# Relative-bias rows replicated by eight DRAM-to-DRAM copies instead of one transfer out of SBUF, in a one-core decoder step

## The chip, the core and the metric

One core of one Trainium2 chip runs the whole program as one launch. The metric is the device time in microseconds; each measured number is one execution, and the program before was run three times: 2370.03, 2372.45 and 2373.29 us, median 2372.45 us.

## What is computed

One layer of a decoder trunk for 1024 prompt tokens and 8 sample tokens (1032 in all), model width 1024. The part that matters here is the first feed-forward step and, much later, a table of biases:

```
h = layer_norm(ALPHA * x + 0.5 * swiglu(x, ffn1_wg, ffn1_wu, ffn1_wd), ln1_g, ln1_b)
...
def swiglu(x, wg, wu, wd):
    return (jax.nn.silu(x @ wg) * (x @ wu)) @ wd
...
bias = rel_bias[t5_bucket(qpos[None, :, None] - idx)].astype(jnp.float32)
logits = logits + bias.transpose(0, 3, 1, 2)
```

`rel_bias` has 32 buckets for each of 8 heads. The bias depends on the distance between query and key alone.

## The kernel before, in words

Everything is computed transposed: features on the partitions, tokens in the free dimension, in three chunks of 344 tokens. Products are made from three matmuls each (high part by high, high by low, low by high), so each weight of 128x1024 (512 KB) is loaded by SP, cast by ScalarE into a high part (L273) and subtracted by VectorE into a low part (L274).

The first feed-forward step runs in two passes. `chunk0` (L416) takes the first 344 tokens through all 22 blocks of the hidden width: `plain` (L369) makes 24 matmuls for the gate (`pg_f`) and 24 for the up projection (`pu_f`), then `down` (L396) multiplies two blocks at a time into eight 128x344 tiles, which VectorE adds to `z` (L407). `chunks12` (L512) then takes the other two chunks together. Beside the first part of `chunk0`, `load_x` (L701) loads x in nine tiles of 128 tokens into three buffers (`xn0` to `xn8`, L710), TensorE transposes each tile (L721), ScalarE and VectorE split the result (L731, L732) and ScalarE copies it into `z` (L736). `load_x` counts the tiles in `g.xb`.

Also in this stretch `bias_rows` (L1253) makes the bias table: TensorE multiplies `rel_bias` with a one-hot matrix (L1262), ScalarE copies the 8x384 result to eight partitions of SBUF (L1264), and one DMA (L1265) writes it to DRAM as `scr`, each head's row of 384 numbers 128 times, 1536 KB. It is read again at L1491, after 1100 us, by an access pattern that shifts each of the 128 rows by one element, which gives the tile of biases of a head.

Order: the Python code runs many generators beside each other, with a clock of its own (`Sched`, L43); a generator yields the time until it wants to go on. Tiles in the pool `ap` share 24 numbered buffers (`A`, L98), which `Free` gives out. Behind that, the framework's scheduler lays down the final order on each engine; it may take an instruction whose inputs are ready ahead of one written earlier. Every engine, SP's DMA queue among them, runs its instructions strictly in that order. `params` (L1943) releases the buffers of the parameters and of the bias.

Of the kernel before, what the change touches and what calls it, by code (L numbers as in the profile page):

```python
# [15 lines left out]
F32 = mybir.dt.float32  # L16
# [69 lines left out]
def bank(g, kind, name):  # L86

    ks = g.banks[kind]
    t = g.ps.tile([P, 512], F32, tag=f"b{ks[g.bi[kind] % len(ks)]}", name=name, bufs=1)
    g.bi[kind] += 1  # L90
    return t
# [6 lines left out]
def A(g, slot, name, dt=F32, n=NTOK):  # L98

    return g.ap.tile([P, n], dt, tag=f"a{slot}", name=name, bufs=1)  # L100
# [1149 lines left out]

def bias_rows(g, rel_bias, oh, scr):  # L1253

    nc = g.nc
    ta = A(g, 20, "bra")
    rb, oht, row = ta[0:32, 0:8], ta[0:32, 8:392], ta[0:8, 400:784]
    nc.sync.dma_start(rb, rel_bias)
    nc.sync.dma_start(oht, oh)
    yield 6.0  # L1260
    ps = bank(g, 'aux', "bt")
    nc.tensor.matmul(ps[0:8, 0:384], rb, oht, start=True, stop=True)  # L1262
    g.s.t += 0.7
    nc.scalar.copy(row, ps[0:8, 0:384])  # L1264
    nc.sync.dma_start(scr, row.unsqueeze(1).broadcast_to((8, 128, 384)))  # L1265


class Pair:
# [615 lines left out]
def trunk(tc, i, o):  # L1884
    nc = tc.nc
    g = G()
    g.nc, g.tc, g.s = nc, tc, Sched()
    s = g.s
# [4 lines left out]
    dp = S_("dp", space=bass.MemoryType.DRAM)  # L1893
# [44 lines left out]
    for j, k in enumerate(ln):  # L1938
        nc.sync.dma_start(prow[8 * j:8 * j + 8], i[k][0].rearrange("(k p) -> k p", p=P))
    nc.sync.dma_start(prow[32:36], i['ret_gn_g'][0].rearrange("(h p) -> h p", p=P))  # L1940
    br = s.add(bias_rows(g, i['rel_bias'], i['oh'], g.scr), 6.0)

    def params():  # L1943

        pp = bank(g, 'aux', "prm")
        nc.tensor.transpose(pp[:, 0:36], prow, g.ident[0:36, 0:36])
        nc.scalar.copy(prm, pp[:, 0:36])
        g.fs.put(21)
        while s.live(br):
            yield 1.0  # L1950
        yield 40.0
        g.fs.put(20)

    def widen():

# [2 lines left out]
        yield 0  # L1958

    s.add(params(), 20.0)  # L1960
    s.add(widen(), 6.0)
    psum = {}
# [31 lines left out]
    h = [None] * NCH  # L1994
# [495 lines left out]
```

## Time and profile before

| | |
|---|---|
| median of three runs | 2372.45 us (2370.03 to 2373.29) |
| the profiled execution | 2370.71 us, span 2368.9 us |
| TensorE busy (share of the span) | 2239.6 us (95%) |
| TensorE weight load busy | 2160.1 us (91%) |
| VectorE busy | 1772.9 us (75%) |
| ScalarE busy | 1076.6 us (45%) |
| GpSimd busy | 361.2 us (15%) |
| DMA moved | 224.40 MB, 95 GB/s on average |

All times of views are microseconds from the start of the span; the execution's own time is 1.81 us longer than the span. A stretch of 40 us near the start is under 2% of the span, so that shares over the whole span say little about it: it has to be read from windows of its own.

### The profile page before, as it was taken

What the parts mean: (1) busy time and instruction counts of PE and PEld (TensorE: products, weight loads), DVE (VectorE), ACT (ScalarE), POOL (GpSimd) and SP (SyncE); (2) the same over time, 40 slices, a digit from 0 to 9 for tenths busy, and PEclk for the clock granted to TensorE, in tenths of its full rate; (3) what the DMA queues carried; (4) which work ended last, traced back from release to release, by engine and by line L of the source; (5) the groups of instructions that cost most, each with busy time, mean ns of one, the idle gap of its engine ahead of it and who ended that gap; (6) DMA issues with size and microseconds to landing.
All of it is one profiled execution on the core that took longest, in us unless ns stands there. A gap on an engine that the chain in (4) does not pass through costs nothing.

```text
span 2368.9 us, 37153 instructions
## 1 busy us (share of the span) xinstructions
PE 2239.6 (95%) x14231; PEld 2160.1 (91%) x14231; DVE 1772.9 (75%) x3780; ACT 1076.6 (45%) x1944; POOL 361.2 (15%) x372
## 2 busy tenths in 40 slices
PE   8899999999999998899899999898999899999996
PEld 7899999999998998888689988787999899999995
DVE  4655688787878588777866678876578788887866
ACT  4433343333334466787466665342345443333331
POOL 0000100000002313454023233223220200000003
PEclk9999999999999999999999999998999999999998
DMA  6644322222222201121321242436644321222211
GB/s 176 208 143 142 119 84 81 81 73 71 81 79 101 71 23 51 50 83 47 90 74 49 57 151 72 146 90 153 190 128 145 110 81 63 90 72 74 87 54 48
DMA packets 239370, 224.40 MB, mean 95 GB/s; under 512 B 13291, under 2 KB 219959, under 8 KB 238423
## 3 DMA queue, kind: packets, MB, share of 16 engines
q1 hardware_dynamic: 234838, 209.36, 29.6%
q0 software_dynamic: 4352, 12.65, 2.3%
q8 instruction: 112, 1.84, 0.3%
q14 instruction: 68, 0.55, 0.1%
HBM read 199.40 MB, written 22.58 MB: 94 GB/s over the span
## 4 chain that ended last, share of the span: by engine, by line
PE 73%; DVE 11%; ACT 7%; DMA 3%; issue 3%; POOL 1%; another core or an unknown queue 1%; SPq 0%; POOLq 0%; DVEq 0%; ACTq 0%
PE pds_f L403 4%; PE pds_f L404 4%; PE pds_f L405 4%; ACT ja L1003 3%; PE pdp_f L403 2%; PE pg_f L171 2%; PE pg_f L169 2%; PE pg_f L170 2%; PE pdp_f L404 2%; PE pdp_f L405 2%; PE ps_f2U L169 2%; PE pu_f L169 2%; PE ps_f2U L170 2%; PE ps_f2U L171 2%; PE ps_f1U L169 2%
## 5 line engine op out<-in xcount | busy, mean ns | idle before, releaser
L407 DVE SCALAR_TENSOR_TENSOR z<-pds_f,z 128x344 f32<-128x344 f32 x320 | 164.4, 515 | 137.9 <-PE pds_f L405 137.4
L403 PE MATMUL pds_f<-gs_f,wh_f1ds 128*128 128x344 f32 x352 | 113.8, 324 | 1.7 <-DVE z L407 1.7
L404 PE MATMUL pds_f<-gs_f,wh_f1ds 128*128 128x344 f32 x352 | 113.1, 321 | 0.0
L403 PE MATMUL pds_f<-gs_f,wh_f2ds 128*128 128x344 f32 x352 | 113.0, 321 | 0.0
L404 PE MATMUL pds_f<-gs_f,wh_f2ds 128*128 128x344 f32 x352 | 113.0, 321 | 0.0
L405 PE MATMUL pds_f<-gs_f,wl_f2ds 128*128 128x344 f32 x352 | 112.8, 321 | 0.0
L405 PE MATMUL pds_f<-gs_f,wl_f1ds 128*128 128x344 f32 x352 | 112.7, 320 | 0.0
L407 DVE SCALAR_TENSOR_TENSOR z<-pdp_f,z 128x344 f32<-128x344 f32 x160 | 79.8, 511 | 43.2 <-PE pdp_f L405 42.6
L1003 ACT ACTIVATE ja<-key,zt 128x1024 bf16<-128x1024 int16 (+5 forms) x90 | 93.8, 1042 | 38.2 <-DVE zt L1014 31.0
L684 POOL TENSOR_TENSOR yt<-yt,lot 128x512 f32<-128x512 f32 (+1 forms) x7 | 7.2, 1040 | 548.5 <-DVE lot L677 530.9
L296 ACT CAST wS_f1G<-ws_f1G 128x512 fp32r<-128x512 f32 x44 | 25.1, 619 | 131.4 <-PE pds_f L404 95.2
L296 ACT CAST wS_f2G<-ws_f2G 128x512 fp32r<-128x512 f32 x44 | 25.2, 618 | 129.5 <-PE pds_f L405 120.9
L1468 ACT CAST p<-pT 128x512 fp32r<-128x512 f32 (+2 forms) x112 | 47.4, 433 | 55.8 <-PE pT L1464 43.4
L574 POOL TENSOR_TENSOR lns_l<-z 128x344 f32<-128x344 f32 x3 | 4.1, 1355 | 440.8 <-DVE z L407 430.3
L403 PEld LDWEIGHTS pds_f<-gs_f,wh_f1ds 128*128 128x128 f32 x352 | 66.5, 189 | 3.0 <-DVE z L407 2.2
L404 PEld LDWEIGHTS pds_f<-gs_f,wh_f1ds 128*128 128x128 f32 x352 | 66.5, 189 | 0.3 <-DVE gs_f L466 0.2
L403 PEld LDWEIGHTS pds_f<-gs_f,wh_f2ds 128*128 128x128 f32 x352 | 66.5, 189 | 0.2 <-ACT gs_f L465 0.2
L405 PEld LDWEIGHTS pds_f<-gs_f,wl_f2ds 128*128 128x128 f32 x352 | 66.5, 189 | 0.0
L404 PEld LDWEIGHTS pds_f<-gs_f,wh_f2ds 128*128 128x128 f32 x352 | 66.4, 189 | 0.0
L405 PEld LDWEIGHTS pds_f<-gs_f,wl_f1ds 128*128 128x128 f32 x352 | 66.5, 189 | 0.0
L403 PE MATMUL pdp_f<-gt_f,wh_f2dp 128*128 128x344 f32 x176 | 57.8, 328 | 3.9 <-issue 2.4
L1469 DVE TENSOR_TENSOR p<-pT,p 128x512 fp32r<-128x512 f32 (+2 forms) x112 | 54.4, 496 | 9.2 <-ACT p L1468 8.0
(806 smaller groups left out, 8729.2 us busy)
## 6 DMA issues: line engine op xcount, KB each, us to landing
wr_f1g<-in_ffn_wg_dram SPq DMA_DIRECT2D x22, 512.0 KB
wr_f1u<-in_ffn_wu_dram SPq DMA_DIRECT2D x22, 512.0 KB
wr_f1dp<-in_ffn_wd_dram SPq DMA_DIRECT2D x22, 512.0 KB
wr_f1G<-in_ffn_wg_dram SPq DMA_DIRECT2D x22, 512.0 KB
wr_f1U<-in_ffn_wu_dram SPq DMA_DIRECT2D x22, 512.0 KB
wr_f1ds<-in_ffn_wd_dram SPq DMA_DIRECT2D x22, 512.0 KB
wr_f2u<-in_ffn_wu_dram SPq DMA_DIRECT2D x22, 512.0 KB
wr_f2g<-in_ffn_wg_dram SPq DMA_DIRECT2D x22, 512.0 KB
```

The lines of the kernel that those rows point to most:

```text
L169: g.nc.tensor.matmul(ps, w[0][:, k, :], x[0][:, k, :], start=first and i == 0, stop=False)
L170: g.nc.tensor.matmul(ps, w[0][:, k, :], x[1][:, k, :], start=False, stop=False)
L171: g.nc.tensor.matmul(ps, w[1][:, k, :], x[0][:, k, :], start=False, stop=last and i == n - 1)
L296: nc.scalar.copy(t[:, 0], src)
L403: g.nc.tensor.matmul(ps, wh[:, o, :], th, start=i == 0, stop=False)
L404: g.nc.tensor.matmul(ps, wh[:, o, :], tl, start=False, stop=False)
L405: g.nc.tensor.matmul(ps, wl[:, o, :], th, start=False, stop=i == len(grp) - 1)
L407: g.nc.vector.scalar_tensor_tensor(out=z, in0=ps, scalar=0.5 / ALPHA, in1=z, op0=OP.mult, op1=OP.add)
L684: nc.gpsimd.tensor_tensor(out=yh, in0=yh, in1=mv[0:n, 0:1].broadcast_to((n, 512)), op=OP.subtract)
L1003: nc.scalar.activation(jk[:, 0:n], key[b], AF.Sign, bias=t[:, j:j + 1], scale=-1.0, accum_out=cnt[:, j:j + 1])
L1468: nc.scalar.copy(ph[:, js, ts], ptv[:, js, ts])
L1469: nc.vector.tensor_tensor(out=pl[:, js, ts], in0=ptv[:, js, ts], in1=ph[:, js, ts].bitcast(F32), op=OP.subtract)
```

## The change

`bias_rows` no longer writes the 1536 KB from SBUF. It stores the 8x384 result once to DRAM (`one`, the new tile `brow`) and then copies, head by head, from DRAM to DRAM: each copy reads one row of `brow` and writes it 128 times into `scr[h]`. In the code the copies come after a loop that waits for the ninth x tile, 12 units of the scheduler's clock apart. The buffer number 20 is now released by `bias_rows` itself.

```diff
-def bias_rows(g, rel_bias, oh, scr):
+def bias_rows(g, rel_bias, oh, one, scr):
...
     nc.scalar.copy(row, ps[0:8, 0:384])
-    nc.sync.dma_start(scr, row.unsqueeze(1).broadcast_to((8, 128, 384)))
+    nc.sync.dma_start(one, row)
+    yield 40.0
+    g.fs.put(20)
+    while g.xb < 9:
+        yield 1.0
+    yield 40.0
+    for h in range(8):
+        nc.sync.dma_start(scr[h], one[h:h + 1, :].broadcast_to((128, 384)))
+        yield 12.0
...
-    br = s.add(bias_rows(g, i['rel_bias'], i['oh'], g.scr), 6.0)
+    s.add(bias_rows(g, i['rel_bias'], i['oh'], dp.tile([8, 384], F32, name="brow"), g.scr), 6.0)
...
         g.fs.put(21)
-        while s.live(br):
-            yield 1.0
-        yield 40.0
-        g.fs.put(20)
+        yield 0
```

SP's queue, from the bias transfer on, before (`wr_f1g4` is the load of the gate weight of block 4, `u` the up and `dp` the down weight, `xn6` the seventh x tile):

```order
L1265 DMA scr_60<-bra_240 1024x1x384
L710 DMA xn6_335<-in_x_prompt_dram 128x1024
L228 DMA wr_f1g4_0_400<-in_ffn1_wg_dram 128x8x128
L228 DMA wr_f1u4_0_425<-in_ffn1_wu_dram 128x8x128
L710 DMA xn7_455<-in_x_prompt_dram 128x1024
L228 DMA wr_f1dp2_0_461<-in_ffn1_wd_dram 128x1024
L228 DMA wr_f1dp3_0_483<-in_ffn1_wd_dram 128x1024
L228 DMA wr_f1g5_0_505<-in_ffn1_wg_dram 128x8x128
L228 DMA wr_f1u5_0_527<-in_ffn1_wu_dram 128x8x128
L228 DMA wr_f1g6_0_548<-in_ffn1_wg_dram 128x8x128
```

and the same place of the same queue with the change:

```order
L1265 DMA brow_179<-bra_241 8x384
L228 DMA wr_f1g4_0_401<-in_ffn1_wg_dram 128x8x128
L710 DMA xn6_336<-in_x_prompt_dram 128x1024
L1272 DMA scr_60<-brow_179 128x384 x2
L228 DMA wr_f1g5_0_506<-in_ffn1_wg_dram 128x8x128
L228 DMA wr_f1u4_0_426<-in_ffn1_wu_dram 128x8x128
L228 DMA wr_f1dp2_0_462<-in_ffn1_wd_dram 128x1024
L228 DMA wr_f1dp3_0_484<-in_ffn1_wd_dram 128x1024
L1272 DMA scr_60<-brow_179 128x384 x3
L710 DMA xn7_456<-in_x_prompt_dram 128x1024
L228 DMA wr_f1u5_0_528<-in_ffn1_wu_dram 128x8x128
L1272 DMA scr_60<-brow_179 128x384 x3
```

The one transfer is gone; the eight copies stand at three places among the loads, all of them ahead of the load of `wr_f1g6`, which is the next row, and of the last x tile.

ScalarE, around the cast of the gate weight of block 4, before (`xt6` is the transposed x tile 6, `z12` the third chunk's `z`):

```order
L736 COPY z12_97<-xt5_1_579 128x4x80
L736 COPY z12_97<-xt6_0_684 128x4x128
L273 CAST wh_f1g4_501<-wr_f1g4_0_400 128x1024
L731 CAST opB22_98<-xt6_1_690 128x4x128
L273 CAST wh_f1u4_523<-wr_f1u4_0_425 128x1024
```

and with the change:

```order
L273 CAST wh_f1u3_480<-wr_f1u3_0_366 128x1024
L273 CAST wh_f1g4_502<-wr_f1g4_0_401 128x1024
L392 CAST gt_f12_347<-s_f12_348 128x344
L273 CAST wh_f1u4_524<-wr_f1u4_0_426 128x1024
L731 CAST xh1_93<-xt4_0_440 128x4x128
```

The cast `wh_f1g4` stood behind the first copy of tile 6; now it stands ahead of tile 4, and the first copy of tile 6 comes 23 rows after it.

VectorE, around the low part of the gate weight of block 6 (`z10<-pdp_f12_0_0` is the first eviction of the second down group), before:

```order
L391 TENSOR_TENSOR s_f14_620<-s_f14_620,pu_f14_653 128x344
L274 TENSOR_TENSOR wl_f1g5_635<-wr_f1g5_0_505,wh_f1g5_634 128x1024
L393 TENSOR_TENSOR gt_f14_619<-s_f14_620,gt_f14_619 128x344
L274 TENSOR_TENSOR wl_f1u5_667<-wr_f1u5_0_527,wh_f1u5_666 128x1024
L407 SCALAR_TENSOR_TENSOR z10_95<-pdp_f12_0_0_701,z10_95 128x344
L407 SCALAR_TENSOR_TENSOR z10_95<-pdp_f12_0_1_709,z10_95 128x344
L274 TENSOR_TENSOR wl_f1g6_718<-wr_f1g6_0_548,wh_f1g6_717 128x1024
```

and with the change:

```order
L393 TENSOR_TENSOR gt_f13_530<-s_f13_531,gt_f13_530 128x344
L274 TENSOR_TENSOR wl_f1u5_668<-wr_f1u5_0_528,wh_f1u5_667 128x1024
L274 TENSOR_TENSOR wl_f1g6_719<-wr_f1g6_0_549,wh_f1g6_718 128x1024
L391 TENSOR_TENSOR s_f14_621<-s_f14_621,pu_f14_654 128x344
L407 SCALAR_TENSOR_TENSOR z10_95<-pdp_f12_0_0_702,z10_95 128x344
```

`wl_f1g6` moved from behind the second eviction to ahead of `s_f14` and of the first.

## Rows read from the trace of the kernel before

**Rows 1.** The page, part 4: shares by engine of the chain that ended last
```profile
PE 73%; DVE 11%; ACT 7%; DMA 3%; issue 3%; POOL 1%; another core or an unknown queue 1%; SPq 0%; POOLq 0%; DVEq 0%; ACTq 0%
```

**Rows 2.** Windows: busy time (instructions) of each engine, clock, DMA share, GB/s
```profile
core 0: us, PE busy (x) PEld busy (x) DVE busy (x) ACT busy (x) POOL busy (x), PEclk, DMA share, GB/s
...
30.00:40.00 10.00, 10.00 (x67) 9.74 (x65) 6.09 (x8) 5.81 (x10) 0.00 (x0) 1.00 0.44 57
...
50.00:62.00 12.00, 6.54 (x45) 6.24 (x43) 1.72 (x4) 2.71 (x8) 0.00 (x0) 0.95 0.44 51
62.00:64.00 2.00, 0.00 (x0) 0.00 (x0) 0.00 (x0) 0.00 (x0) 0.00 (x0) 0.50 0.93 304
64.00:72.00 8.00, 6.22 (x24) 5.41 (x25) 3.64 (x5) 5.08 (x7) 0.00 (x0) 0.56 0.98 319
```

**Rows 3.** Waits of TensorE, 0 to 200 us: total, times, longest
```profile
PE xt L721 <- DMA xn<-in_x_prompt_dram: 12.6, 2, 8.1
```

**Rows 4.** Chain that ended last, 28 to 75 us: start, us, what
```profile
30.80 33.75 DMA xn<-in_x_prompt_dram
...
66.39 0.96 ACT wh_f1g L273
...
67.38 1.24 DVE wl_f1g L274
```

**Rows 5.** DMA issues, 29.3 to 64.5 us
```profile
scr<-bra SPq DMA_DIRECT2D x1, 1536.0 KB
```

**Rows 6.** Timeline of SP's DMA queue: start, us to issue, line, out<-in
```profile
29.30 0.81 SPq L1265 DMA_DIRECT2D scr<-bra  x1
30.80 9.14 SPq L710 DMA_DIRECT2D xn<-in_x_prompt_dram  x1
40.03 4.33 SPq L228 DMA_DIRECT2D wr_f1g<-in_ffn_wg_dram  x1
44.45 16.51 SPq L228 DMA_DIRECT2D wr_f1u<-in_ffn_wu_dram  x1
61.05 3.37 SPq L710 DMA_DIRECT2D xn<-in_x_prompt_dram  x1
```

**Rows 7.** Timeline of ScalarE: in brackets the idle time before, and what ended it
```profile
65.81 0.58 ACT L736 COPY z<-xt 128x512 f32<-128x512 f32 x1 [9.57 <-PE xt L721]
```

**Rows 8.** Timeline of TensorE around the stall
```profile
52.68 1.04 PE L721 MATMUL xt<-ident,xn 128*128 128x128 f32 x8
53.47 0.40 PE L169 MATMUL pu_f<-xh,wh_f1u 128*128 128x344 f32 x1
...
56.07 0.32 PE L170 MATMUL pu_f<-xl,wh_f1u 128*128 128x344 f32 x1
56.23 0.31 PE L171 MATMUL pu_f<-xh,wl_f1u 128*128 128x344 f32 x1
...
67.40 0.65 PE L169 MATMUL pg_f<-xh,wh_f1g 128*128 128x344 f32 x1 [0.78 <-ACT wh_f1g L273]
...
70.83 0.41 PE L169 MATMUL pg_f<-xh,wh_f1g 128*128 128x344 f32 x1
71.08 0.32 PE L170 MATMUL pg_f<-xl,wh_f1g 128*128 128x344 f32 x1
```

**Rows 9.** SP's queue and windows: loads of LayerNorm rows; a store to `zscr`
```profile
2290.69 0.33 SPq L2419 DMA_DIRECT2D ln_g_rows<-in_ln_g_dram  x1
2292.57 0.33 SPq L2419 DMA_DIRECT2D ln_b_rows<-in_ln_b_dram  x1
...
2291.00:2296.50 5.50, 5.50 (x37) 5.50 (x37) 2.18 (x5) 1.56 (x4) 0.00 (x0) 1.00 0.60 192
...
764.00:767.00 3.00, 3.00 (x21) 3.00 (x21) 2.94 (x3) 2.96 (x5) 0.00 (x0) 1.00 0.99 411
```

**Rows 10.** Timeline of VectorE: split of a down weight, last eviction of the first group
```profile
33.68 1.22 DVE L274 TENSOR_TENSOR wl_f1dp<-wr_f1dp,wh_f1dp 128x1024 fp32r<-128x1024 f32 x1
...
48.47 0.52 DVE L407 SCALAR_TENSOR_TENSOR z<-pdp_f,z 128x344 f32<-128x344 f32 x1 [0.43 <-PE pdp_f L405]
```

**Rows 11.** Waits of TensorE at the first LayerNorm, 704 to 760 us
```profile
PE pv_l L635 <- DVE lns_l L625: 2.5, 1, 2.5
PE pds_f L403 <- DVE z L407: 1.7, 1, 1.7
```

## The prediction, made before the change was run

> **What bounds the kernel now.** I read the page first. The chain that ended last is 73% TensorE [rows 1], so whatever keeps TensorE from its next matmul moves the end, provided that nothing later absorbs it. Next I read the windows over the place of the change. From 30 to 50 us TensorE is full; in 50:62 it is busy for 6.54 of 12 us, in 62:64 not at all, and in 64:72 for 6.22 of 8 us at a granted clock of 0.56 [rows 2]. The waits of TensorE name the cause: transposes of x (L721) behind the DMA into `xn`, 8.1 us in one piece [rows 3]. The chain of waits says the same: one piece of 33.75 us, from 30.80 on, is that DMA [rows 4]. 33.75 us for 512 KB is not what such a load needs, so I looked at what was ahead of it in SP's queue. It is the transfer that the diff replaces: `scr<-bra`, 1536 KB [rows 5], issued at 29.30; the load of `xn6` behind it took 9.14 us to issue, the next two 4.33 and 16.51 us [rows 6]. In 30:40 and 50:62 the DMA engines show a share of only 0.44 and 57 and 51 GB/s [rows 2]: some seven of sixteen engines' time, for 33 us (1573 kB at 49 to 51 GB/s is 31 to 32 us). So a slow transfer on a part of the engines holds up every load that has a share on those engines. ScalarE passes the delay on: it runs in order, `z<-xt` (the copy of x tile 6) stood there waiting for 9.57 us [rows 7], and the cast of the weight that TensorE needed next stands behind it.
>
> **What the stall costs.** The last matmul ahead of it starts at 56.23; at a pitch of 0.16 us (56.07 to 56.23) TensorE would be free for the next at 56.39. The first matmul with the fast pitch again starts at 71.08 [rows 8]. In these 14.69 us lie eight transposes of x tile 6 and ten matmuls (those that start from 67.40 to 70.83). At the full clock the eight transposes take 0.79 us (52.68 to 53.47, for tile 5) and the ten matmuls 1.6 us. The stall with its aftermath, slow clock included, is therefore worth 14.69 - 0.79 - 1.6 = **12.3 us**.
>
> **The change, part by part.**
> - Removed: the 1536 KB transfer. Added: a store of 12 KB into `brow` and eight copies of 196.6 kB, DRAM to DRAM. All of them are issued by SP; TensorE, VectorE and ScalarE get no new instruction. One store and eight copies are eight DMAs more on SP, 0.3 to 0.8 us each to issue by the plain issues in [rows 6, 9], 3 to 6 us on a queue that sits waiting for buffers in between: nothing.
> - The first copy has to wait until `brow` has landed. What stands behind it on SP: the second copy, then the load of `f1g5`, whose buffer VectorE reads until 34.9 (33.68 + 1.22) [rows 10]. From the store at 29.3 that leaves 5 us; I cost this wait at nothing.
> - Moved: x tile 6 and the gate weight of f=4 now stand ahead of all copies. They are issued near 30 to 31 and, with no slow transfer ahead, land before 36 at the 300 GB/s that loads reach in 62:72 [rows 2]. TensorE wants the weight at 56.4, tile 6 a little later. On ScalarE the cast of that weight now stands 23 places ahead of the first copy of tile 6, so the two are uncoupled as well. The 12.3 us go, if nothing else is late.
> - What is late next: the copies do not wait for x, whatever the loop in the code says. In the order they stand at three places, two after tile 6, three before tile 7, three before `f1g6`. `f1g6` is the load to watch, because VectorE now splits it (`wl_f1g6`) ahead of `s_f14` and of the first eviction of the second down group; before, it came after two of these evictions. Without the stall, f=4 takes 48 matmuls and eight transposes from 56.4, 8.5 us, so down starts near 64.9. It has two banks and asks for the first eviction 12 matmuls later, at 66.8. Until then VectorE has the eviction (0.52), `s_f14`, as long, and the split (1.22) [rows 10] to do, and ScalarE the cast (0.96 [rows 4]): `f1g6` must have landed by about 63.5.
> - When it lands: the first copy goes at about 32. From then the engines move eight copies of c us each and seven loads of 524 kB (`f1g5`, `f1u4`, `dp2`, `dp3`, tile 7, `f1u5`, `f1g6`), 1.75 us each at 300 GB/s, 12.3 us; 2 us for landing. That is 46 + 8c, if all queue without a gap. Its own buffer is not free before the first down group ends (last eviction at 48.47 [rows 10]). The stall is 46 + 8c - 63.5: none up to c = 2.2, all 12.3 us given back at **c = 3.7**, which is 53 GB/s.
>
> **The price of a copy.** The trace has no DRAM to DRAM transfer. From below in speed: the old transfer moved 49 GB/s on about half of the engines. If each engine was the limit, sixteen would move 98 GB/s, c = 2.0. From above: one DRAM row read for 128 destinations stands in the trace, the loads of the LayerNorm rows, 2 x 524 kB in 5.5 us at 192 GB/s on average, c = 1.0; DRAM is written at 411 GB/s where `zscr` is stored [rows 9], so writing to DRAM is no brake. c = 0.5 would be the fastest. I take **c = 1.0**: the LayerNorm rows are the nearest, since source pattern and spread are the same and only the destination differs. With it, or with 2.0, no stall is left.
>
> [...]
>
> **The sum.** 2370.71 (the profiled execution) - 12.3 = 2358.4. The median of the runs lies 1.74 above that execution, so I expect **2360** where the runs centre. Two smaller things I cost at zero. The scheduler has also reordered some rows between 250 and 830 us, above all at the first LayerNorm: two evictions now stand ahead of the subtraction there, which may remove a wait of 1.7 us, while the matmul of the mean comes a few rows later, and `wl_kr` moves in before the second chunk's LayerNorm, 1.2 us in a place where TensorE waits 2.5 us for that LayerNorm [rows 11]. Together -1.7 to +2.5. And behind that place the order of all engines is as before, with no fixed times in it, so that a start gained early is kept.
>
> **The rivals.**
> 1. Another wait takes the stall's place: copies between c = 2.2 and 3.7, or VectorE and ScalarE held by a split that came early. At c = 3.0 the stall is 6.5 us, the time 2366.5. For it: three engines run in order, and the copies stand among the loads. Against it: nothing in the rows is that slow unless it touches eight partitions. 0.12.
> 2. The gain is lost at the first LayerNorm seam or later, and the time is 2370 to 2374. For it: VectorE bounds that seam in part [rows 11]. Against it: its inputs come from TensorE and move with it. 0.07.
> 3. Slower: all sixteen engines read one 1536-byte row of DRAM, 128 times per copy, and write DRAM at once. If that goes at 33 GB/s, c = 6, the stall is 30.5 us and the time 2391. It decides from c = 3.7 on: below that the change wins, above c = 4.3 it loses by more than 0.2%. Then the old transfer would have been better, since it left half of the engines free. Against it: the 192 GB/s above. 0.07.
> 4. That the change doesn't do what it says is partly certain: the copies are not held until the two-chunk pass but stand beside the last x tiles, as the order shows. This gives no time of its own; it is why c matters, and is in 1 and 3.
>
> **The numbers.** The forecast has 0.74: 2354.5 (the seam's 1.7 gained, the profiled execution's level and the spread of the runs) to 2363. Range: with most of rival 1 it reaches to 2367.0. A measurement of this kernel tells some 0.2% (4.7 us) from no change: faster is below 2367.7, slower above 2377.2. Faster: 0.74 and 0.10 of rival 1, 0.84. Same: the rest of rival 1 and rival 2, 0.09. Slower: rival 3, 0.07.
>
> **What would show it.** Right: the piece of 33.75 us is gone from the chain, TensorE is full in 50:72 with a clock of 1.00, tile 6 is issued in about 0.4 us, DMA rates of 200 GB/s and more where the copies run, each gone in about 1 us. Rival 1 or 3: TensorE waits between 60 and 95 us, with VectorE at the split of `f1g6` or `f1u5` behind a DMA, and long issues on SP after a copy. Rival 2: full windows up to 100 us and the time lost at the first LayerNorm. A stretch 50:72 that is empty as before would prove that the old transfer was not the cause, and the prediction wrong.

## The result, and the profile after

| | median us | ratio to before |
|---|---|---|
| before (5 runs) | 2372.45 (2370.03 to 2377.16) | |
| changed (5 runs) | 2356.01 (2351.40 to 2359.13) | 0.9928 [0.9913, 0.9943] |
| changed, once more beside other kernels (6 runs) | 2352.57 (2350.75 to 2356.56) | 0.9917 [0.9903, 0.9930] |

The change is faster, by 13.5 to 20.6 us in the first comparison (the interval times 2372.45), against 12.3 predicted for the stall; 2356.01 lies inside the forecast (2354.5 to 2363) and 4 us below its centre. The profiled execution took 2352.69 us, its span is 2350.9.

The windows of [rows 2], now of the changed kernel (40 to 50 us added):

```profile
30.00:40.00 10.00, 10.00 (x67) 9.73 (x66) 5.70 (x7) 5.80 (x10) 0.00 (x0) 1.00 0.90 261
40.00:50.00 10.00, 10.00 (x68) 9.98 (x67) 7.88 (x14) 5.24 (x8) 0.00 (x0) 1.00 0.98 326
50.00:62.00 12.00, 12.00 (x81) 11.98 (x81) 7.27 (x10) 7.61 (x15) 0.00 (x0) 1.00 0.55 159
62.00:64.00 2.00, 2.00 (x14) 2.00 (x14) 1.29 (x2) 0.32 (x1) 0.00 (x0) 1.00 0.68 223
64.00:72.00 8.00, 8.00 (x55) 7.98 (x54) 5.70 (x10) 4.03 (x6) 0.00 (x0) 1.00 0.46 133
```

TensorE is full from 30 to 72 us at a granted clock of 1.00, where it had been busy for 6.54 of 12, 0 of 2 and 6.22 of 8 us. The DMA engines, at 0.44 before in 30:40 and 50:62, work at 0.90 and 0.98 while the copies run. The waits of TensorE from 0 to 200 us have one piece left for x, at the very start of the program, of the two in [rows 3]:

```profile
PE xt L721 <- DMA xn<-in_x_prompt_dram: 4.6, 1, 4.6
```

SP's queue ([rows 6] before): tile 6 needs 0.34 us to issue instead of 9.14, and no issue up to 57 us lasts longer than 3.75 us.

```profile
29.95 0.30 SPq L1265 DMA_DIRECT2D brow<-bra  x1
30.34 0.37 SPq L228 DMA_DIRECT2D wr_f1g<-in_ffn_wg_dram  x1
31.46 0.34 SPq L710 DMA_DIRECT2D xn<-in_x_prompt_dram  x1
32.33 1.24 SPq L1272 DMA_DIRECT2D scr<-brow  x2
...
36.74 3.75 SPq L228 DMA_DIRECT2D wr_f1dp<-in_ffn_wd_dram  x2
40.55 1.76 SPq L1272 DMA_DIRECT2D scr<-brow  x3
...
44.36 2.28 SPq L1272 DMA_DIRECT2D scr<-brow  x3
49.85 0.39 SPq L228 DMA_DIRECT2D wr_f1g<-in_ffn_wg_dram  x1
```

The last of these is the load of f1g6. Its cast on ScalarE has no idle time before it:

```profile
61.28 1.04 ACT L273 CAST wh_f1g<-wr_f1g 128x1024 fp32r<-128x1024 f32 x1
```

**Where the time came from.** All three traces hold 14231 matmuls on TensorE. The table takes the n-th of each and subtracts the start after from the start before: the lead in us at that point (time of before in the first column).

| us, before | 55 | 77 | 258 | 354 | 701 | 834 | 1587 | 1630 | 1903 | 2352 |
|---|---|---|---|---|---|---|---|---|---|---|
| changed | -0.6 | 11.6 | 11.8 | 12.5 | 12.5 | 15.1 | 15.1 | 18.4 | 17.9 | 18.5 |
| changed, second profile | -0.8 | 11.4 | 11.6 | 12.3 | 12.3 | 14.5 | 11.3 | 16.2 | 14.0 | 14.6 |

Three steps come back in both: 12.2 us at the stall, 0.7 near 295, 2.5 and 2.2 at the first LayerNorm, 15 in all. Behind 834 us, where the order of all engines is that of before, the two differ by up to 4 us: that belongs to single executions and is read into nothing.

The waits of TensorE at the first LayerNorm, 690 to 835 us, before ([rows 11] has two more waits of this stretch):

```profile
PE pkt L1124 <- DVE zt L916: 1.4, 1, 1.4
PE sc L942 <- DVE qT L1136: 1.4, 1, 1.4
```

and after, in the same stretch:

```profile
PE pv_l L635 <- DVE lns_l L625: 2.9, 2, 2.5
PE pw_ki L170 <- DVE h1l L650: 1.5, 1, 1.5
PE pkt L1124 <- DVE zt L916: 0.6, 1, 0.6
PE pw_ki L169 <- DVE qst L893: 0.2, 1, 0.2
```

The wait of 1.7 us for an eviction into `z` [rows 11] and that of 1.4 us for `qT` are gone, the one for `zt` fell from 1.4 to 0.6 us, and the 2.5 us for `lns_l` stayed as they were.

### The profile page after: what moved, and what is told of

Same layout as the page of the kernel before. It is cut to its first block, busy times and chain, and to the rows that moved or that the text cites. A ratio compares the mean times of both kernels' runs of the same rounds, so it can differ in the third digit from the quotient of the medians.

```text
span 2350.9 us, 37167 instructions
## 1 busy us (share of the span) xinstructions
PE 2234.5 (95%) x14231; PEld 2160.9 (92%) x14231; DVE 1770.0 (75%) x3780; ACT 1078.0 (46%) x1944; POOL 363.2 (15%) x372
## 3 DMA queue, kind: packets, MB, share of 16 engines
q1 hardware_dynamic: 234974, 209.37, 29.3%
## 4 chain that ended last, share of the span: by engine, by line
PE 74%; DVE 11%; ACT 7%; issue 3%; DMA 2%; POOL 2%; SPq 0%; POOLq 0%; DVEq 0%; ACTq 0%
PE pds_f L403 5%; PE pds_f L404 5%; PE pds_f L405 5%; ACT ja L1003 3%; PE pdp_f L403 2%; PE pdp_f L405 2%; PE pdp_f L404 2%; PE pg_f L169 2%; PE pg_f L170 2%; PE pg_f L171 2%; PE pu_f L169 2%; PE pu_f L170 2%; PE pu_f L171 2%; PE ps_f2U L169 2%; PE ps_f2U L170 2%
```

## Experiments

Times are medians of 5 to 11 runs, each with its ratio to the runs of before beside it. Lead is read as in the table above; the lead at the stall is what it rises by between 55 and 77 us.

**1. One transfer out of SBUF, rows spread over partitions** (`spread`)

```diff
-    rb, oht, row = ta[0:32, 0:8], ta[0:32, 8:392], ta[0:8, 400:784]
-    nc.sync.dma_start(rb, rel_bias)
+    rb, oht, row = ta[0:32, 800:928], ta[0:32, 8:392], ta[:, 400:784]
+    nc.gpsimd.memset(rb, 0.0)
+    nc.sync.dma_start(rb[:, 0:128:16], rel_bias)
...
-    nc.sync.dma_start(scr, row.unsqueeze(1).broadcast_to((8, 128, 384)))
+    nc.sync.dma_start(scr, row[0:128:16].unsqueeze(1).broadcast_to((8, 128, 384)))
```

> The kernel before, with its one transfer out of SBUF at its old place ahead of x tile 6; only the eight source rows lie on partitions 0, 16, ... 112 instead of 0 to 7. Theory A (eight neighbouring partitions are the slow thing): the packets of 1536 bytes, which took a mean of 0.44 x 16 x 33 us / 1024 = about 0.22 us each before, get shorter than 0.12 us, the transfer is gone in under 18 us, x tile 6 lands before it is wanted at 56.4, the stall of 12.5 us goes and the time is 2358 to 2361. Theory B (any one transfer of eight rows out of SBUF is slow, wherever they lie): rate of 45 to 60 GB/s in 32 to 60 us as before, time 2369 to 2376.

Measured: 2363.33 us, 0.9967 [0.9955, 0.9979]; packets of 0.114 us on average (0.215 before), the last one at 48 us, 17 us after the first. Windows of 1 us in which this transfer runs nearly alone, of before:

```profile
33.00:34.00 1.00, 1.00 (x8) 1.00 (x7) 1.00 (x3) 1.00 (x3) 0.00 (x0) 1.00 0.43 49
```

and of `spread`:

```profile
33.00:34.00 1.00, 1.00 (x9) 1.00 (x8) 1.00 (x3) 1.00 (x2) 0.00 (x0) 1.00 0.45 103
```

The same share of the engines (0.45, and 0.43 before) moves twice as much (103 GB/s, and 49 before). The slow thing was where the rows lay. But the lead at the stall is 9.9 us and not 12.2, and the time 2 us above the band: theory A was right on the rate and gave too much for it.

**2. Sixteen rows instead of eight** (`spread16`, against `spread`)

```diff
     nc.sync.dma_start(rb[:, 0:128:16], rel_bias)
+    nc.sync.dma_start(rb[:, 8:128:16], rel_bias)
...
-    nc.sync.dma_start(scr, row[0:128:16].unsqueeze(1).broadcast_to((8, 128, 384)))
+    nc.sync.dma_start(scr.rearrange("h (s r) m -> (h s) r m", s=2), row[0:128:8].unsqueeze(1).broadcast_to((16, 64, 384)))
```

> As the run that spread the eight source rows, with the same order on all engines, but each head's row lies on two partitions (sixteen rows, 8 partitions apart) and is written 64 times from each. Theory A (the eight rows give work to about half of the DMA engines, the neighbouring partitions slow each packet): a DMA share above 0.8 and 180 GB/s or more while it runs, gone in 9 us or less instead of 16 to 18. Theory C (what that run still lost, 2 us of waits of TensorE for wh_f1g4 and wl_f1g4, is the order on ScalarE, whose cast stands behind the first copy of x tile 6): the start gained by 100 us stays at 8 to 9.5 us and the time at 2361 to 2365, however fast the transfer is. Rival (the loads were still late): 11 us or more gained by 100 us, 2357 to 2361.

Measured: 2361.77 us, 0.9953 [0.9941, 0.9966]; 195 to 212 GB/s while it runs, gone after 8 us. Twice the speed bought nothing at the stall: the lead there is 8.3 us (9.9 in `spread`). Windows of `spread16`:

```profile
36.00:37.00 1.00, 1.00 (x7) 0.99 (x7) 1.00 (x1) 1.00 (x3) 0.00 (x0) 1.00 0.92 204
...
50.00:62.00 12.00, 10.14 (x66) 9.58 (x65) 4.68 (x7) 6.27 (x14) 0.00 (x0) 0.98 0.06 15
```

its waits of TensorE, 20 to 330 us:

```profile
PE pg_f L169 <- ACT wh_f1g L273: 1.2, 1, 1.2
PE pg_f L171 <- DVE wl_f1g L274: 0.7, 1, 0.7
```

and its ScalarE:

```profile
57.43 0.58 ACT L736 COPY z<-xt 128x512 f32<-128x512 f32 x1 [0.78 <-PE xt L721]
57.91 1.05 ACT L273 CAST wh_f1g<-wr_f1g 128x1024 fp32r<-128x1024 f32 x1
```

In 50:62 the DMA engines are idle (0.06), every load has landed, and TensorE still waits: the cast of f1g4 stands behind the copy of tile 6, whose transposes are TensorE's last work ahead of it. That is the order, not the transfer. Theory C held.

The two waits of 1.2 and 0.7 us are the same in `spread`. The 1.6 us between their leads are granted clock, which fell behind the waits in `spread16` alone. `spread`:

```profile
62.00:64.00 2.00, 2.00 (x15) 2.00 (x14) 1.08 (x2) 1.40 (x2) 0.00 (x0) 1.00 1.10 317
64.00:72.00 8.00, 8.00 (x52) 7.93 (x52) 6.11 (x9) 5.67 (x7) 0.00 (x0) 1.00 0.93 269
```

and `spread16`, 57 matmuls in the time of 67:

```profile
62.00:72.00 10.00, 10.00 (x57) 10.00 (x57) 5.64 (x7) 6.55 (x9) 0.00 (x0) 0.86 0.93 290
```

**3. The place of the rows, or the engines at work?** (`step4` against `spread`, `near16` against `spread16`)

Two readings of 1 and 2 differ in the rate that they expect here, and not in the time: the place of the rows sets the rate, whatever share of the engines is at work, or the engines at work set it (theory E).

```diff
-    nc.sync.dma_start(rb[:, 0:128:16], rel_bias)
+    nc.sync.dma_start(rb[:, 0:32:4], rel_bias)
...
-    nc.sync.dma_start(scr, row[0:128:16].unsqueeze(1).broadcast_to((8, 128, 384)))
+    nc.sync.dma_start(scr, row[0:32:4].unsqueeze(1).broadcast_to((8, 128, 384)))
```

> The kernel before with its one transfer of eight rows out of SBUF; the rows lie on partitions 0, 4, ... 28 instead of 0, 16, ... 112 as in the first run that spread them (101 GB/s, a DMA share of 0.44, packets of 0.114 us) or 0 to 7 as before (49 GB/s). The order on all engines is that of the first spread run. [...] Theory E (half of the engines, each at 0.11 us per packet, set the rate): 95 to 105 GB/s as with 16 apart. The time is 2361 to 2365 by both, since the wait that is left there is the order on ScalarE.

```diff
-    nc.sync.dma_start(rb[:, 0:128:16], rel_bias)
-    nc.sync.dma_start(rb[:, 8:128:16], rel_bias)
+    nc.sync.dma_start(rb[:, 0:16:2], rel_bias)
+    nc.sync.dma_start(rb[:, 1:16:2], rel_bias)
...
-    nc.sync.dma_start(scr.rearrange("h (s r) m -> (h s) r m", s=2), row[0:128:8].unsqueeze(1).broadcast_to((16, 64, 384)))
+    nc.sync.dma_start(scr.rearrange("h (s r) m -> (h s) r m", s=2), row[0:16].unsqueeze(1).broadcast_to((16, 64, 384)))
```

> The kernel before with sixteen source rows (each head's row twice) on the neighbouring partitions 0 to 15, instead of 8 apart as in the run that reached 200 GB/s with a DMA share of 0.98 and packets of 0.112 us. The order on all engines is that of that run. [...] Theory E (the engines set it): about 200 GB/s and packets of 0.11 us. The time is 2360 to 2365 by both.

Measured: `step4` 2366.43 us, 0.9960 [0.9946, 0.9974]; `near16` 2363.86 us, 0.9958 [0.9944, 0.9972]. The kernel before lay at 2376.12 beside them, so that the gains are 9.7 and 12.3 us, near the 8.0 and 10.5 of 1 and 2 (`step4`'s median itself is 1.4 us above the expected band). Their leads at the stall are 8.3 and 9.9 us, with the same two waits; the clock fell to 0.50 in 62 to 64 us in `step4`, as in `spread16`, and stayed at 1.00 in `near16`. Windows of `step4`:

```profile
33.00:34.00 1.00, 1.00 (x8) 1.00 (x7) 1.00 (x3) 1.00 (x2) 0.00 (x0) 1.00 0.53 200
```

and of `near16`:

```profile
36.00:37.00 1.00, 1.00 (x7) 0.84 (x6) 1.00 (x3) 1.00 (x5) 0.00 (x0) 1.00 0.87 98
```

At half of the engines' time 200 GB/s are moved from partitions 4 apart; at nearly all of it, 98 from neighbours. Theory E, with 95 to 105 and about 200 GB/s, fell both times: in these runs the place set the rate. (Shares and rates are of 1 us in which the transfer runs nearly alone; packets are those of 1536 bytes, over the whole transfer.)

| source | rows | share of engines | GB/s | mean packet us |
|---|---|---|---|---|
| partitions 0 to 7 (before) | 8 | 0.43 | 49 | 0.215 |
| 0, 16, ... 112 | 8 | 0.45 | 103 | 0.114 |
| 0, 4, ... 28 | 8 | 0.53 | 200 | 0.071 |
| 0 to 15 | 16 | 0.87 | 98 | 0.212 |
| 0, 8, ... 120 | 16 | 0.92 | 204 | 0.112 |
| DRAM, one transfer (4) | 8 | 0.54 | 203 | 0.066 |

Eight rows gave 49, 103 or 200 GB/s by their places alone, sixteen 98 or 204. What it is about the places that sets the rate, no run shows.

**4. One DRAM to DRAM transfer** (`dram_one`)

```diff
...
-    nc.sync.dma_start(scr, row.unsqueeze(1).broadcast_to((8, 128, 384)))
+    nc.sync.dma_start(one, row)
+    nc.sync.dma_start(scr, one.unsqueeze(1).broadcast_to((8, 128, 384)))
...
```

> The kernel before with brow stored and read again as in the change, but by one DRAM to DRAM transfer of 1024 rows in the place of eight copies, and with no wait for x in the code. In the order it stands behind the load of f1g4 and x tile 6; from 110 us on all engines' order is that of the kernel before, the first LayerNorm too. Theory A (the source is what counts, not the number of transfers): no stall in 50 to 72 us, start gained there 11.8 us or more; the reorder at the first LayerNorm, which gave 2 to 2.5 us in the profile of the change, is missing, so the time is 2357.5 to 2361. Rival (the cut into eight matters, one transfer of eight rows still takes some eight engines): 80 to 110 GB/s over 15 us or more, and a wait for f1u4 or the down weights behind it, time 2361 to 2370. Rival (the LayerNorm reorder is worth nothing by itself): time 2354 to 2357.

Measured: 2365.60 us, 0.9973 [0.9962, 0.9984], slower than all that was expected by theory A. Its windows:

```profile
37.00:38.00 1.00, 1.00 (x8) 1.00 (x8) 0.75 (x1) 1.00 (x3) 0.00 (x0) 1.00 0.54 203
...
62.00:64.00 2.00, 0.25 (x3) 0.02 (x1) 0.69 (x1) 1.24 (x3) 0.00 (x0) 1.00 0.00 0
```

and its ScalarE:

```profile
61.42 0.46 ACT L389 ACTIVATE s_f<-pg_f 128x344 f32<-128x344 f32 x1 [4.09 <-PE pg_f L171]
61.85 0.59 ACT L736 COPY z<-xt 128x512 f32<-128x512 f32 x1
62.34 0.59 ACT L731 CAST opB<-xt 128x512 fp32r<-128x512 f32 x1
63.69 0.59 ACT L736 COPY z<-xt 128x512 f32<-128x512 f32 x1 [0.76 <-DVE opB L732]
64.17 1.05 ACT L273 CAST wh_f1u<-wr_f1u 128x1024 fp32r<-128x1024 f32 x1
```

The transfer ran at 203 GB/s, no DMA is under way at 62 to 64 us, and TensorE waits 3.0 us for the cast of f1u4, which the order had put behind tile 6. (The rival saw half of the engines rightly, but no load was late.) The first LayerNorm, in the order of before, still has its wait of 1.6 us for `z` and 1.3 for `qT`, and the lead falls there from 5.6 to 5.1. So the 2.2 to 2.5 us that the change gains there come with its order. All profiles bear that out: in the five that keep the old order there (`spread`, `spread16`, `step4`, `near16`, `dram_one`) the lead falls by 0.1 to 2.5 us between 701 and 834 us, and in the five without the wait for `z` (the two of the change, `double`, `quad`, `sbrow`) it rises by 2.2 to 3.3.

**5. The old transfer behind f1g4 and tile 6** (`old_later`)

```diff
+    while g.xb < 9:
+        yield 1.0
+    yield 40.0
     nc.sync.dma_start(scr, row.unsqueeze(1).broadcast_to((8, 128, 384)))
```

> The kernel before with the one transfer out of SBUF unchanged, but with the waits of the change ahead of it in the code: in the order f1g4 and x tile 6 now stand ahead of it, f1u4, x tile 7 and the down weights behind it. Theory A (the slow transfer itself holds up what shares its engines): it lasts 30 us or more as before, from 32 to beyond 62; f1u4, wanted near 60, comes at 62 to 67, TensorE stalls for 5 to 13 us in 50 to 75 us, time 2362 to 2373. Rival (the place in the queue is what the change gained by, with x tile 6 and f1g4 ahead): full windows, time 2354 to 2361.

Measured: 2367.33 us, 0.9982 [0.9972, 0.9991]; packets of 0.211 us. Its SP queue:

```profile
32.27 0.81 SPq L1268 DMA_DIRECT2D scr<-bra  x1
37.34 6.52 SPq L228 DMA_DIRECT2D wr_f1u<-in_ffn_wu_dram  x1
43.96 16.15 SPq L710 DMA_DIRECT2D xn<-in_x_prompt_dram  x1
```

and the longest wait of TensorE after 20 us:

```profile
PE pu_f L169 <- ACT wh_f1u L273: 7.7, 1, 7.7
```

ScalarE shows that here the load itself is late:

```profile
68.74 1.04 ACT L273 CAST wh_f1u<-wr_f1u 128x1024 fp32r<-128x1024 f32 x1 [4.63 <-DMA wr_f1u<-in_ffn_wu_dram]
```

The place alone moves the stall from one weight to the next: 7.7 us at f1u4, where `dram_one` has 3.0 behind a cast in the same place, and a lead at the stall of 2.8 us instead of 12.2. The rival on the place falls.

**6. Four times and twice the copies** (`quad`, `double`)

```diff
-        nc.sync.dma_start(scr[h], one[h:h + 1, :].broadcast_to((128, 384)))
+        for _ in range(4):
+            nc.sync.dma_start(scr[h], one[h:h + 1, :].broadcast_to((128, 384)))
```

> The changed kernel with each of the eight copies made four times over (32 copies, 6.3 MB); the order on TensorE, VectorE, ScalarE and GpSimd is that of the change. 13 copies instead of 8 stand ahead of the load of f1g6. By the prediction's working f1g6 lands at 46 + 13c and is wanted at 63.5. With copies of 0.6 us (1024 x 0.074 us / 16 / 8, from the packets in the profile of the change) no stall, time within 3 us of the change's 2356. If a copy really costs 2 us behind its issue: 8 us of stall or more, time 2364 or more, TensorE waiting behind the split of f1g6 or f1u6.

(`range(2)` in `double`)

> The changed kernel with each copy made twice (16 copies). With four times as many (32) the stretch 30 to 90 us was full, and 10 us were lost at 94 us, where the load of f1g7 stood behind ten copies in SP's queue. With twice as many the order stays that of the change, at most three copies are added ahead of f1g6 and the rest behind it. Theory (the copies hide in the slack of the loads, and cost nothing until that is used up): no wait over 1 us before 700 us, time within 2 us of the changed kernel's. Rival (each copy costs something): a third of what 24 more copies cost, 3 us.

Measured: `quad` 2367.10 us, 0.9986 [0.9977, 0.9995]; `double` 2355.37 us, 0.9922 [0.9907, 0.9937], with one wait of TensorE between 20 and 700 us:

```profile
PE ps_f1U L169 <- DVE pc_f1G L469: 0.2, 1, 0.2
```

Its median is 2.8 us above that of the changed kernel beside it (2352.57): beyond the 2 us of the theory and near the 3 of the rival, but the two intervals overlap almost wholly, so the times do not decide. The lead does, up to 834 us: 15.0 there, with 15.1 and 14.5 in the two profiles of the change. `quad` missed its band: full until 90 us, then

```profile
PE pdp_f L403 <- DVE z L407: 10.0, 1, 10.0
```

with SP's queue ahead of it

```profile
72.80 15.19 SPq L1273 DMA_DIRECT2D scr<-brow  x10
88.04 0.59 SPq L228 DMA_DIRECT2D wr_f1g<-in_ffn_wg_dram  x1
```

and ScalarE

```profile
94.95 1.04 ACT L273 CAST wh_f1g<-wr_f1g 128x1024 fp32r<-128x1024 f32 x1 [9.82 <-DMA wr_f1g<-in_ffn_wg_dram]
```

Ten copies in a row take 15.19 us to issue, and the load behind them (it is f1g8; the expectation of `double` names it wrongly) comes 10 us late. VectorE passes that on, its split standing ahead of an eviction. It is the prediction's rival 1, at another load than the one I had watched. Eight and sixteen copies cost no lead up to 834 us; thirty-two give back 12 us (lead 11.8 at 90 us, -0.3 at 110), the wait of 10.0 and a lower clock behind it (0.74 in 90 to 110 us): a slack, not a price per copy.

**7. Cut head by head, but out of SBUF** (`sbrow`)

```diff
-    rb, oht, row = ta[0:32, 0:8], ta[0:32, 8:392], ta[0:8, 400:784]
+    rb, oht, row = ta[0:32, 0:8], ta[0:32, 8:392], g.ms.tile([8, 384], F32, name="brw")
...
-        nc.sync.dma_start(scr[h], one[h:h + 1, :].broadcast_to((128, 384)))
+        nc.sync.dma_start(scr[h], row[h:h + 1, :].unsqueeze(1).broadcast_to((1, 128, 384)))
```

> The changed kernel with its eight copies cut head by head as they are, but each from its row in SBUF, one partition at a time, instead of from DRAM (brow is still stored, not read). The framework then lays the copies out further apart (one before the load of f1u4, the others from 75 to 200 us) and puts the cast of f1u4 behind the copies of x tile 6 on ScalarE, as in the run with one DRAM to DRAM transfer. Theory A: the source is what is slow: packets of 150 ns or more, a copy of 196 kB lasts 4 us or more. Rival (cutting it is what helps): packets of 60 to 90 ns as in the change. Either way the wait for wh_f1u4 of about 3 us near 62 us stays, 7 to 10 us of start gained by 110 us, time 2360 to 2367; a copy that lasts over 20 us would bring 8 us of waits or more instead.

Measured: 2387.06 us, 1.0058 [1.0040, 1.0076]: slower than before, and 20 us beyond the band. Windows:

```profile
37.00:38.00 1.00, 1.00 (x8) 1.00 (x8) 0.87 (x1) 1.00 (x3) 0.00 (x0) 1.00 0.81 28
160.00:165.00 5.00, 2.85 (x17) 2.33 (x16) 3.22 (x3) 4.24 (x5) 0.00 (x0) 1.00 0.00 0
```

A copy out of one partition moves 28 GB/s at a share of 0.81 in that window and takes 4.6 to 7.2 us from its first packet to its last: cutting does not help (49 GB/s uncut, in the kernel before), the source does. But the loss is elsewhere. Up to 110 us its lead is that of `dram_one` (5.7, below the 7 to 10 expected); at 258 us it is -12.1, at 354 us -17.6. In 160 to 165 us no DMA runs and TensorE waits for casts on ScalarE: there it is the order that the framework made for these copies. How much of the 23 us between 110 and 354 us is order, and how much the copies, is not shown.

**8. The changed kernel again** (`after_again`, no edit)

> The changed kernel once more, beside the others. Its profile tells which differences between two profiles come back: the 12.5 us at 56 to 75 us, 2.0 us at the first subtraction of the first LayerNorm and 2.1 us at 818 to 830 us should; the 3 us that the first profile had gained between 1597 and 1706 us, where the order of all engines is that of before, should come out differently. Time 2354 to 2358.

Measured: 2352.57 us, 0.9917 [0.9903, 0.9930], 1.4 us below the band. The lead came back as expected at all three places. The step near 1600 us, expected to be chance, came again (11.3 to 16.2; 3.2 in `spread`, but -0.3 in `step4`, all with one order there), and 3.8 us were lost just ahead of it, which the first profile had not: the lead ended at 14.6 instead of 18.5 us.

No run beat the changed kernel.

## Why the prediction was right, and what it missed

- **The stall.** Predicted 12.3 us, measured 12.2 in both profiles (lead -0.6 to 11.6, -0.8 to 11.4). Every sign named for it is there.
- **Its cause** was named only in half. "So a slow transfer on a part of the engines holds up every load": right, and shown by 1 to 3 with the place unchanged, but that is worth 8 to 10 us (8.3 to 9.9 of lead at the stall, 8 to 12 us in the runs). The prediction mentioned the cast that "now stands 23 places ahead" as a second safety; it is a second cause. 2 and 4 have a fast transfer and a cast behind tile 6 (f1g4, f1u4), and their leads at the stall, 8.3 and 6.8 us, are 4 and 5 us short of the change's: 1.9 and 3.5 us are waits for that cast and its low part, most of the rest is the lower clock behind them (0.86 in 62 to 72 us of `spread16`, 0.79 in 64 to 72 us of `dram_one`).
- **The price of a copy.** c = 1.0 was taken; the packets of 1536 bytes last 0.074 us on average from 32 to 50 us, 1024 x 0.074 / 16 = 4.7 us of all engines, c = 0.6, near the lower bound. "If each engine was the limit" is the branch that falls: the place of the rows set the rate (3: 200 GB/s at a share of 0.53, 98 at 0.87). A c of 2.5 would by the sum have given a stall of 2.5 us and a time near 2363, the upper end of the forecast; no run shows copies out of DRAM that slow. They overlap with each other and with the loads (0.98 and 326 GB/s in 40 to 50 us), the change has no such stall, and sixteen copies in `double` cost no lead up to 834 us. The "2 us for landing" in the sum was an estimate that no row gives; the changed kernel shows 2.1 us for the store of `brow`, whose issue ends at 30.25 and for which the first copy waits until 32.33.
- **f1g6** was issued at 49.85, after the last eviction of the first group as reckoned, and its cast at 61.28 waited for no DMA; `quad` shows that the kind of stall feared is real, at four times the copies.
- **What was mis-sized:** "Two smaller things I cost at zero", -1.7 to +2.5 us. They gave 2.2 to 2.5 at the first LayerNorm and 0.7 near 295 us, of which 0.3 is a wait for `pc_f1G` that fell from 0.5 to 0.2. Of the two signs in that term only the good one came: the wait of 1.7 us went, as named, another of 1.4 us for `qT` and most of one for `zt` went with it, and the 2.5 us wait that `wl_kr` might have lengthened is 2.5 as before. With 12.2 + 0.7 + 2.4 the sum would have been 15.3, 2357.1 on the median, 1.1 us above the first measurement.
- **Left open.** The second comparison gains 19.7 us (16.6 to 23.0), 15.3 are placed. Behind 834 us single profiles of the same order differ by 4 us, so the rest can't be placed. The 2.2 to 2.5 us at the first LayerNorm may be too little, since the one profile of before lost less there than the five others with its order. And the change leaves another loss of the stall's size alone: in 1580 to 1640 us TensorE is idle for 10.7 to 10.9 us in all three profiles.
- **Rivals.** 2 and 3 did not come; 1 did not at eight copies. 4 was right: the copies run at 32 to 51 us, not in the two-chunk pass.

## What to carry to other kernels

Here a transfer out of eight neighbouring partitions, at 49 GB/s, delayed far more than itself: the load of tile 6 behind it took 9.14 us to issue (0.34 in the change), and TensorE lost 8 to 10 us by it. Look for a low DMA share (0.44 here) together with long issues on the queue, then try the source spread over partitions 4 apart (200 GB/s here) or read from DRAM (203 GB/s). When an edit changes what a scheduler thinks of a transfer, it reorders other engines too, and here that was worth 5 to 7 of the 15 us that could be placed: cost the reorder by the waits that it removes, and not at zero. A second kernel with the same transfer but another order, or the reverse, separates the two.

## What the runs showed of the hardware

How fast the rows were read out of SBUF changed with their places at the same number of rows: eight rows on partitions 0 to 7 gave 49 GB/s, on 0, 4, ... 28 they gave 200 with little more of the engines at work (0.53 against 0.43). A larger share of the engines did not by itself move more: sixteen rows on 0 to 15 took 0.87 of the engines for 98 GB/s with packets of 0.212 us, eight rows 16 apart 0.45 for 103 with 0.114. A single DRAM row read 128 times per copy was no hot spot: 0.066 us per packet in `dram_one` and 0.074 in the change, among the shortest of all (0.071 from partitions 4 apart). The granted clock after the same two waits of 1.2 and 0.7 us differed between the runs: it stayed at 1.00 in `spread` and `near16` and was at 0.50 in 62 to 64 us in `spread16` and `step4`, whose lead at the stall is 1.6 us smaller (8.3 against 9.9).
